# A hybrid encoder block: PSUM tiles of the w_o products, the rounding of the first key weights, and the place of the parameter transposes

## The chip, the cores and the metric

The kernel runs on one core of one Trainium2 chip. The metric is the device time of one execution in microseconds, lower is better. A core has TensorE (PE, matmuls; PEld is its loading of the stationary operand), VectorE (DVE), ScalarE (ACT), GpSimd (POOL) and SyncE (SP, which issues most of the DMAs). The engines run side by side, each works through its own queue in order, and they wait for each other on semaphores. TensorE accumulates in PSUM, in eight banks of 128 x 512 fp32.

## What is computed

One encoder block on x of 512 tokens by 1024 channels, all in fp32. Cut to what matters here:

```python
h = rmsnorm(x, norm1_w)
proj = h @ w_in              # pooling | q | k | v | z | beta, decay (the gate columns) | merge gates
...                          # pooling branch and gated delta rule over 8 heads, both directions
merged = sigmoid(g_pool) * y_pool + sigmoid(g_dn) * y_dn
x = x + merged @ w_o
h2 = rmsnorm(x, norm2_w)
u = dwconv_centered(h2 @ ffn_up, ffn_conv_w, ffn_conv_b)
gate, val = split(u)
return rmsnorm(x + (silu(gate) * val) @ ffn_down, final_norm_w)
```

## The kernel before

**Matmuls in three parts.** Every fp32 operand of the large products is split into a rounded high part (fp32r) and the rest, a low part. `mm3` (L388 to L391) issues three matmuls for each k-step of 128 rows: high x high (L389), and the two mixed ones (L390, L391). Weights come by DMA into a raw tile; in `weights` (L399 to L422) ScalarE rounds it (L411, one copy of 128 x 1024) and GpSimd subtracts, in two halves of 128 x 512 (L415).

**The order.** No engine's order is written out by hand. The kernel declares tasks (A for ScalarE, V for VectorE, G for GpSimd, M for TensorE, L for loads, Z for none), each with a cost, the names it reads and writes, and a key. A planner (L38) plays them through by costs and due keys and hands each engine its queue; after that the queues are fixed. Names such as `whi:k0#1` are parts of a buffer. Buffers of one tag form a ring: `pp` and `ds` have three PSUM banks each, `oo` is one tile of two banks (`banks2`, L307). Waits between engines are derived afterwards from the tiles that the instructions touch: instructions of different engines on one PSUM tile are kept in the order of the program.

**The head.** The first norm goes over four tiles of 128 tokens (`norm_transpose`, L526): ScalarE squares and sums a tile of x (L534), takes the root (L537), VectorE takes the reciprocal (L539) and scales it in two halves (L545), TensorE transposes each half into a `ds` bank (L556, four transposes), ScalarE rounds it into h_hi (L560), and VectorE subtracts into h_lo (L564), which frees the bank. The gate columns (L466, L467, L469) and the first two key heads (ps_k) are computed in two halves of 256 tokens, so that they can start on the first two tiles. Between these stand `par_turn` (L512), which transposes four blocks of small parameters (convolution weights, scales) into a `ds` bank, and `par_keep` (L517), by which ScalarE keeps them (cw, fw, small).

**The w_o stage.** merged @ w_o is computed by seven products of half size in place of eight (products 1, 2, 6, 5, 3, 7, 4 in this order). A product has 256 tokens, in two halves j of 128, and 512 rows (four k-steps) of 512 columns: 2 x 4 x 3 matmuls. Each half is accumulated in one PSUM bank and then added by VectorE to one or two quarters of x (`wplus`, L1776). Products 1 and 6 are also kept by ScalarE as wu (`wkeep`, L1783), product 1's for adding it into product 6 (`wmore`, L1788), product 6's for sums that GpSimd makes. The left operands are splits of merged (ms, L1566, L1570, L1657, L1661), the right ones splits of sums of w_o's quarters (L1617, L1630, L1633). Between product 4's k-steps stand the transposes of the second norm (pt_b, L1743), whose tiles come by L1727, L1729, L1730, L1733 and L1737. Behind it comes the FFN (ps_up).

The banks of the seven products, before, by `wname` and `wmm` (L1755 to L1766): products 1, 6, 3 and 4 share one tile wo of the ring `oo`, made once, with half j in its bank j; the halves of 2, 5 and 7 are tiles of the ring `pp`.

Of the kernel before, what the change touches and what calls it, by code (L numbers as in the profile page):

```python
# [205 lines left out]
def ca(n):  # L206
    return 0.22 + n * 0.00082
# [6 lines left out]
def cp(n):  # L214
    return 0.17 + n * 0.0023
# [12 lines left out]
def hybrid_block(  # L228
# [23 lines left out]
    pe, act, dve, pool, sp = nc.tensor, nc.scalar, nc.vector, nc.gpsimd, nc.sync  # L252
# [16 lines left out]
    def with_table(tab, fn):  # L269
        def run():  # L270
            if table["now"] != tab:
                table["now"] = tab
                if TABLES[tab]:
                    act.preload_act_table_set(TABLES[tab])
            fn()

        return run

    def A(cost, fn, r=(), w=(), key=0.0, tab=None):
        add("act", cost, with_table(tab, fn) if tab else fn, r, w, key, tab)  # L280
# [4 lines left out]
    def G(cost, fn, r=(), w=(), key=0.0, after=()):  # L285
        add("pool", cost, fn, r, w, key, after=after)

    def M(cost, fn, r=(), w=(), key=0.0, n=6):
        add("pe", cost, fn, r, w, key, n=n)

    def L(kb, fn, r=(), w=(), key=0.0, after=(), land=Planner.LAND, issue=Planner.ISSUE, eng="sp"):
        add(eng, issue, fn, r, w, key, kb=kb, after=after, land=land)
# [6 lines left out]
    FEED, EVICT, CHAIN = -3e6, -2e6, -1e6  # L299

    def f32(ap):
        return ap.bitcast(F32)

    def bank(tag, name):
        return psum.tile([P, 512], F32, tag=tag, bufs=RINGS[tag], name=name)

    def banks2(name, shape=(P, 2, 512)):  # L307
        return psum.tile(list(shape), F32, tag="oo", bufs=RINGS["oo"], name=name)
# [79 lines left out]
    def mm3(ps, ahi, alo, bhi, blo, first, last):  # L388
        pe.matmul(ps, ahi, bhi, start=first, stop=False)  # L389
        pe.matmul(ps, ahi, blo, start=False, stop=False)  # L390
        pe.matmul(ps, alo, bhi, start=False, stop=last)  # L391
# [3 lines left out]
    def next_unit():  # L395
        unit["n"] += 1
        return unit["n"] * 100.0

    def weights(src, kt, n, name, u, feed=None, more=0.0):  # L399
        feed = FEED + u if feed is None else feed  # L400

        b = {}

        def load():
            b["raw"] = wpool.tile([P, kt, n], F32, tag="wraw", bufs=RINGS["raw"], name=f"wr_{name}")
            sp.dma_start(b["raw"], src)

        def hi():
            b["hi"] = wpool.tile([P, kt, n], F32R, tag="whi", bufs=RINGS["whi"], name=f"wh_{name}")
            b["lo"] = wpool.tile([P, kt, n], F32R, tag="wlo", bufs=RINGS["wlo"], name=f"wl_{name}")  # L410
            act.copy(b["hi"], b["raw"])  # L411

        def lo(i):
            sl = slice(i * kt // 2, (i + 1) * kt // 2)
            pool.tensor_tensor(out=b["lo"][:, sl], in0=b["raw"][:, sl], in1=f32(b["hi"][:, sl]), op=ALU.subtract)  # L415

        whi, wlo = f"whi:{name}", f"wlo:{name}"
        L(kt * n * P * 4 / 1024, load, w=[f"raw:{name}"], key=feed)
        A(ca(kt * n), hi, r=[f"raw:{name}"], w=[whi, f"{wlo}#0"], key=feed)
        for i in range(2):  # L420
            G(cp(kt * n / 2) + more, lambda i=i: lo(i), r=[f"raw:{name}", whi], w=[f"{wlo}#{i}"], key=feed)
        return b, whi, wlo  # L422

    def job(src, kt, xs, xr, name, halves=False, pair=False, feed=None, more=0.0, at=None, turn=0):


        n = src.shape[1]
        u = next_unit()
        src = src.rearrange("(k p) c -> p k c", p=P)
        box = {}  # L430
        if pair:
            def load():
                box["raw"] = wpool.tile([P, kt, n], F32, tag="wraw", bufs=RINGS["raw"], name=f"wr_{name}")
                sp.dma_start(box["raw"], src)

            def split():
                w = box["hi"] = wpool.tile([P, kt, 2 * n], F32R, tag="whi", bufs=RINGS["whi"], name=f"wp_{name}")
                act.copy(w[:, :, 0:n], box["raw"])

            def split2():  # L440
                w = box["hi"]
                pool.tensor_tensor(out=w[:, :, n:], in0=box["raw"], in1=f32(w[:, :, 0:n]), op=ALU.subtract)

            whi = f"whi:{name}"
            wlo = whi
            L(128, load, w=[f"raw:{name}"], key=FEED + u)
            A(ca(kt * n), split, r=[f"raw:{name}"], w=[whi], key=FEED + u)
            G(cp(kt * n), split2, r=[f"raw:{name}"], w=[whi], key=FEED + u)
        else:
            if at:  # L450
                wk, wn = at(src, name, feed)
            else:
                wb, whi, wlo = weights(src, kt, n, name, u, feed, more)
                wk = lambda k: (wb["hi"][:, k, :], wb["lo"][:, k, :])
                wn = lambda k: [whi, f"{wlo}#{0 if k < kt // 2 else 1}"]
        pp = f"pp:{name}"

        def mmk(k, a, b):
            if "ps" not in box:
                box["ps"] = bank("pp", f"ps_{name}")  # L460
            xhi, xlo = xs(k)
            if pair:
                w = box["hi"]
                both = (box["ps"][: 2 * n, a:b], w[:, k, :], xhi[:, a:b])
                if k < kt - 1:
                    pe.matmul(*both, start=(k == 0), stop=False)  # L466
                pe.matmul(box["ps"][:n, a:b], w[:, k, 0:n], xlo[:, a:b], start=False, stop=False)  # L467
                if k == kt - 1:
                    pe.matmul(*both, start=False, stop=True)  # L469
                return  # L470
            mm3(box["ps"][:n, a:b], *wk(k), xhi[:, a:b], xlo[:, a:b], k == 0, k == kt - 1)

        spans = [(0, S)] if not halves else [(0, S // 2), (S // 2, S)]
        for i, (a, b) in enumerate(spans):
            for k in range(kt):
                M((MM3 if not pair else 0.46) / len(spans), lambda k=k, a=a, b=b: mmk(k, a, b),
                  r=([whi] if pair else wn(k)) + xr(k, a, b), w=[pp], key=u + (50 + turn) * i + k, n=4 if pair else 6)
        return box, pp, u
# [5 lines left out]
    par = {}  # L484
# [12 lines left out]
    def par_load(i):  # L497
        if "r" not in par:
            par["r"] = [pools["st"].tile([n, P], F32, name=f"par{i}") for i, n in enumerate((120, 88, 88, 5))]
        r = par["r"]  # L500
        (
            lambda: sp.dma_start(r[0], qkv_conv_w[0].rearrange("k (c p) -> (k c) p", p=P)),
            lambda: sp.dma_start(r[1], ffn_conv_w[0, 0:2].rearrange("k (c p) -> (k c) p", p=P)),
            lambda: sp.dma_start(r[2][0:44, :], ffn_conv_w[0, 2].rearrange("(c p) -> c p", p=P)),
            lambda: sp.dma_start(r[2][44:88, :], ffn_conv_b[0].rearrange("(c p) -> c p", p=P)),
            lambda: sp.dma_start(r[3][0:4, :], pool_scale[0].rearrange("(c p) -> c p", p=P)),
            lambda: sp.dma_start(r[3][4:5, :], dn_norm_w),
            lambda: sp.dma_start(ea, a_log[0].partition_broadcast(P)),
            lambda: sp.dma_start(dtb, dt_bias[0].partition_broadcast(P)),
        )[i]()  # L510
# [943 lines left out]
        )  # L1454
    for i in range(8):
        L(32, lambda i=i: par_load(i), w=[f"par#{i}"], key=FEED + 310 + i)
    M(0.6, par_turn, r=[f"par#{i}" for i in range(6)], w=["ds:par"], key=CHAIN, n=8)
    A(0.35, lambda: par_keep(0), r=["ds:par"], w=["cw"], key=CHAIN)
    A(0.6, lambda: par_keep(1), r=["ds:par"], w=["small"], key=CHAIN + 900)
    G(1.5, make_edges, w=["edges"], key=5000)  # L1460
# [51 lines left out]
    for c2 in range(KD // 2):  # L1512
# [9 lines left out]
      w=["wr"], after=["h"])  # L1522
# [63 lines left out]
    for t in range(NT):  # L1586
        L(512, lambda t=t: sp.dma_start(x2[t], xt[t * P : (t + 1) * P, :]), r=["pool:xp"], w=[f"xr{t}#0", f"xr{t}#1"],
          key=unit["n"] * 100, after=[f"pp:do{1 + t}"])
    L(512, lambda: sp.dma_start(pools["n2b"], norm2_w[0].partition_broadcast(P)), r=["pool:xp"], w=["n2b"],
      key=unit["n"] * 100, after=["pp:do5"])  # L1590
# [16 lines left out]
    for i, (kk, n) in enumerate(((0, 0), (0, 1), (2, 1), (1, 0), (1, 1), (3, 1), (2, 0), (3, 0))):  # L1607
        L(512, lambda n=n, kk=kk: wo_load(n, kk), r=["wr"], w=[f"wr{n}{2 * kk}", f"wr{n}{2 * kk + 1}"],
          key=WORK + u_w0, after=[f"pp:{pace[i]}"])
# [143 lines left out]
    wacc = {}  # L1753

    def wname(p, j):  # L1755
        return f"oo:wo#{j}" if p in (1, 6, 3, 4) else f"pp:wo{p}{j}"

    def wmm(p, k, j):
        name = wname(p, j)
        if p == 1 and "oo" not in wacc:  # L1760
            wacc["oo"] = banks2("wo")
        if name[0] == "p" and k == 0:
            wacc[name] = bank("pp", f"ps_wo{p}{j}")
        wacc[p, j] = wacc["oo"][:, j, :] if name[0] == "o" else wacc[name]
        a, ts_ = wsets[p], slice(j * P, (j + 1) * P)
        mm3(wacc[p, j], a[:, k, 0, ts_], a[:, k, 1, ts_], *wslot[p, k], k == 0, k == QK - 1)  # L1766

# [171 lines left out]
    for c in range(NF):  # L1939
        b = {}  # L1940
        for j in range(2):
            box, pp, u = first_jobs.get((c, j)) or up_job(c, j)
# [16 lines left out]
        else:  # L1959
            i = c - HK  # L1960
# [255 lines left out]
```

## Time and profile before

| | |
|---|---|
| median of 3 runs | 878.43 us (878.30 to 879.63) |
| the profiled execution's own time | 877.32 us |
| its span on the core | 875.5 us |
| TensorE busy | 863.7 us, 99% |
| VectorE, ScalarE, GpSimd busy | 592.0, 476.1, 530.1 us |
| granted TensorE clock, mean | 0.996 |
| moved by DMA | 138.09 MB, 158 GB/s |

The page shows one execution, by engine and by line of the kernel (L411 is line 411). In a row of the timeline stand the start and the duration in us, the engine, line and operation, the tiles as out<-in, shapes, and in brackets the idle time of the engine before it with what ended it. A row of the waits reads: who waited, for whom, us in total, times, longest. TensorE's matmuls overlap, so that 0.39 us is how long one is under way, and the distance between starts is what one costs.

### The profile page before, as it was taken

What the parts mean: (1) busy time and instruction counts of PE and PEld (TensorE: products, weight loads), DVE (VectorE), ACT (ScalarE), POOL (GpSimd) and SP (SyncE); (2) the same over time, 40 slices, a digit from 0 to 9 for tenths busy, and PEclk for the clock granted to TensorE, in tenths of its full rate; (3) what the DMA queues carried; (4) which work ended last, traced back from release to release, by engine and by line L of the source; (5) the groups of instructions that cost most, each with busy time, mean ns of one, the idle gap of its engine ahead of it and who ended that gap; (6) DMA issues with size and microseconds to landing.
All of it is one profiled execution on the core that took longest, in us unless ns stands there. A gap on an engine that the chain in (4) does not pass through costs nothing.

```text
span 875.5 us, 13895 instructions
## 1 busy us (share of the span) xinstructions
PE 863.7 (99%) x5051; PEld 730.5 (83%) x5051; DVE 592.0 (68%) x1040; ACT 476.1 (54%) x806; POOL 530.1 (61%) x459
## 2 busy tenths in 40 slices
PE   8999999999999999999999999999999999999997
PEld 7888888888888887889888789888888888888886
DVE  5756597367568897555676894656654555569996
ACT  6688544336858544345866664444443333455664
POOL 3445554324546654244597993778777887567663
PEclk9999999999999999999999999999999999999998
DMA  7365447304245463224898004666667666365553
GB/s 210 97 196 145 122 122 165 111 26 133 73 120 153 130 149 89 67 73 140 297 316 281 1 25 127 226 199 205 207 218 236 207 199 208 133 216 182 182 175 148
DMA packets 165512, 138.09 MB, mean 158 GB/s; under 512 B 23662, under 2 KB 133051, under 8 KB 165444
## 3 DMA queue, kind: packets, MB, share of 16 engines
q1 hardware_dynamic: 160706, 135.62, 50.5%
q10 hardware_dynamic: 4738, 1.58, 0.8%
q8 instruction: 40, 0.66, 0.3%
q14 instruction: 28, 0.23, 0.1%
HBM read 113.03 MB, written 24.15 MB: 157 GB/s over the span
## 4 chain that ended last, share of the span: by engine, by line
PE 97%; DVE 2%; ACT 0%; issue 0%; DVEq 0%
PE ps_up L389 9%; PE ps_up L391 9%; PE ps_up L390 9%; PE dn L391 4%; PE dn L389 4%; PE dn L390 4%; PE ps_k L389 2%; PE ps_gd L389 2%; PE ps_k L391 2%; PE ps_k L390 2%; PE pw L1167 2%; PE ps_q L391 2%; PE ps_q L389 2%; PE ps_v L390 2%; PE ps_gd L391 2%; PE ps_z L391 2%
## 5 line engine op out<-in xcount | busy, mean ns | idle before, releaser
L415 POOL TENSOR_TENSOR wl_up<-wr_up,wh_up 128x512 fp32r<-128x512 f32 x86 | 112.0, 1323 | 53.2 <-ACT wh_up L411 53.2
L389 PE MATMUL ps_up<-h_hi,wh_up 128*128 128x512 f32 (+1 forms) x360 | 136.8, 380 | 0.0
L390 PE MATMUL ps_up<-h_lo,wh_up 128*128 128x512 f32 (+1 forms) x360 | 136.6, 380 | 0.0
L391 PE MATMUL ps_up<-h_hi,wl_up 128*128 128x512 f32 (+1 forms) x360 | 136.6, 380 | 0.0
L1930 DVE SCALAR_TENSOR_TENSOR c<-ps_up,fw,c 128x511 f32<-128x511 f32 x88 | 66.0, 750 | 99.7 <-ACT c L1924 98.0
L2118 POOL TENSOR_TENSOR w_dn<-wr_dn,w_dn 128x512 fp32r<-128x512 f32 x44 | 65.8, 1509 | 28.8 <-ACT w_dn L2115 27.4
L391 PEld LDWEIGHTS ps_up<-h_hi,wl_up 128*128 128x128 f32 x360 | 67.7, 188 | 12.9
L390 PEld LDWEIGHTS ps_up<-h_lo,wh_up 128*128 128x128 f32 x360 | 67.7, 188 | 12.8
L389 PEld LDWEIGHTS ps_up<-h_hi,wh_up 128*128 128x128 f32 x360 | 67.7, 188 | 12.7
L411 ACT CAST wh_up<-wr_up 128x1024 fp32r<-128x1024 f32 x43 | 45.2, 1052 | 59.0 <-PE ps_up L390 23.4
L1915 POOL TENSOR_TENSOR tp<-tp 128x512 f32<-128x512 f32 x44 | 61.7, 1401 | 11.8 <-DMA tp<-in_ffn_down_dram 7.6
L2115 ACT CAST w_dn<-wr_dn 128x512 fp32r<-128x512 f32 x69 | 42.4, 621 | 29.5 <-PE dn L391 20.5
L390 PE MATMUL dn<-w_dn,as 128*128 128x512 f32 x141 | 54.2, 385 | 0.0
L389 PE MATMUL dn<-w_dn,as 128*128 128x512 f32 x141 | 54.2, 384 | 0.0
L391 PE MATMUL dn<-w_dn,as 128*128 128x512 f32 x141 | 54.2, 384 | 0.0
L1884 DVE TENSOR_TENSOR as<-a,as 128x512 fp32r<-128x512 f32 (+1 forms) x41 | 40.6, 1015 | 0.1
L1880 ACT CAST as<-a 128x512 fp32r<-128x512 f32 (+1 forms) x41 | 21.5, 534 | 33.4 <-DVE a L1950 29.8
L415 POOL TENSOR_TENSOR wl_k<-wr_k,wh_k 128x512 fp32r<-128x512 f32 x16 | 20.2, 1287 | 30.3 <-ACT wh_k L411 30.3
L1924 ACT ACTIVATE c<-ps_up,fw 128x512 f32<-128x512 f32 x44 | 33.9, 770 | 4.9 <-PE ps_up L391 4.9
L415 POOL TENSOR_TENSOR wl_v<-wr_v,wh_v 128x512 fp32r<-128x512 f32 x16 | 21.3, 1352 | 22.7 <-ACT wh_v L411 22.7
L415 POOL TENSOR_TENSOR wl_gp<-wr_gp,wh_gp 128x512 fp32r<-128x512 f32 x16 | 21.9, 1390 | 20.8 <-ACT wh_gp L411 20.8
L1952 ACT ACTIVATE c<-c 128x512 f32<-128x512 f32 x22 | 13.9, 632 | 33.0 <-DVE c L1930 33.0
(406 smaller groups left out, 2536.2 us busy)
## 6 DMA issues: line engine op xcount, KB each, us to landing
wr_up<-in_ffn_up_dram SPq DMA_DIRECT2D x44, 512.0 KB, 3.9
tp<-in_ffn_down_dram SPq DMA_DIRECT2D x22, 512.0 KB, 5.2
t_scr<-tp SPq DMA_DIRECT2D x44, 256.0 KB, 2.8
wr_dn<-t_scr SPq DMA_DIRECT2D x20, 512.0 KB, 3.7
wr_dn<-in_ffn_down_dram SPq DMA_DIRECT2D x15, 512.0 KB, 3.6
x<-in_x_dram SPq DMA_DIRECT2D x8, 512.0 KB, 5.4
wr_k<-in_w_in_dram SPq DMA_DIRECT2D x8, 512.0 KB, 4.7
wr_z<-in_w_in_dram SPq DMA_DIRECT2D x8, 512.0 KB, 3.8
```

The costliest lines, as they stand in the source:

```text
L389: pe.matmul(ps, ahi, bhi, start=first, stop=False)
L390: pe.matmul(ps, ahi, blo, start=False, stop=False)
L391: pe.matmul(ps, alo, bhi, start=False, stop=last)
L411: act.copy(b["hi"], b["raw"])
L415: pool.tensor_tensor(out=b["lo"][:, sl], in0=b["raw"][:, sl], in1=f32(b["hi"][:, sl]), op=ALU.subtract)
L1880: act.copy(sets[p][:, i : i + n, 0, :], src())
L1884: dve.tensor_tensor(out=w[:, :, 1, :], in0=src(), in1=f32(w[:, :, 0, :]), op=ALU.subtract)
L1915: G(cp(512), lambda o=o, x=x, y=y: pool.tensor_tensor(out=w(*o), in0=w(*x), in1=w(*y), op=ALU.subtract), r=[n(*x), n(*y)], w=[n(*o)], key=u)
L1924: act.activation(b[j], box["ps"], AF.Identity, scale=fw[:, 1, ci : ci + 1], bias=fw[:, 3, ci : ci + 1])
L1930: dve.scalar_tensor_tensor(out=y[:, lo:hi], in0=box["ps"][:, lo + sh : hi + sh], scalar=fw[:, k, ci : ci + 1], in1=y[:, lo:hi], op0=ALU.mu ...
L2115: act.copy(b["w"][:, 0, :], raw["t"][:, j, :])
L2118: eng.tensor_tensor(out=b["w"][:, 1, :], in0=raw["t"][:, j, :], in1=f32(b["w"][:, 0, :]), op=ALU.subtract)
```

## The change

Three things are edited. (1) The first key head's weights (k0) are rounded by GpSimd and not by ScalarE, in two halves, each followed by its subtraction; matmuls of the first four k-steps need the first halves alone. (2) The parameter transposes must wait until the first half of the last tile of the first norm is rounded (`h#hi30`). (3) Each half of each of the seven products has a PSUM tile of its own: 2, 5, 7 in `pp` as before, the first halves of 3 and 4 in `oo`, all others in `ds`.

```diff
         def hi():
             b["hi"] = wpool.tile([P, kt, n], F32R, tag="whi", bufs=RINGS["whi"], name=f"wh_{name}")
             b["lo"] = wpool.tile([P, kt, n], F32R, tag="wlo", bufs=RINGS["wlo"], name=f"wl_{name}")
-            act.copy(b["hi"], b["raw"])
+            if not first:
+                act.copy(b["hi"], b["raw"])
+
+        def hi_part(i):
+            sl = slice(i * kt // 2, (i + 1) * kt // 2)
+            pool.tensor_copy(out=b["hi"][:, sl], in_=b["raw"][:, sl])
...
+        first = name == "k0"
...
-        A(ca(kt * n), hi, r=[f"raw:{name}"], w=[whi, f"{wlo}#0"], key=feed)
+        (Z if first else A)(*(() if first else (ca(kt * n),)), hi, r=[f"raw:{name}"], w=[whi, f"{wlo}#0"], key=feed)
         for i in range(2):
-            G(cp(kt * n / 2) + more, lambda i=i: lo(i), r=[f"raw:{name}", whi], w=[f"{wlo}#{i}"], key=feed)
+            if first:
+                G(cp(kt * n / 2), lambda i=i: hi_part(i), r=[f"raw:{name}"], w=[f"{whi}#{i}"], key=feed)
+            G(cp(kt * n / 2) + more, lambda i=i: lo(i), r=[f"raw:{name}", f"{whi}#{i}" if first else whi], w=[f"{wlo}#{i}"], key=feed)
...
-                wn = lambda k: [whi, f"{wlo}#{0 if k < kt // 2 else 1}"]
+                wn = lambda k: [f"{whi}#{0 if k < kt // 2 else 1}" if name == "k0" else whi, f"{wlo}#{0 if k < kt // 2 else 1}"]
...
-    M(0.6, par_turn, r=[f"par#{i}" for i in range(6)], w=["ds:par"], key=CHAIN, n=8)
+    M(0.6, par_turn, r=["h#hi30", *(f"par#{i}" for i in range(6))], w=["ds:par"], key=CHAIN, n=8)
...
     def wname(p, j):
-        return f"oo:wo#{j}" if p in (1, 6, 3, 4) else f"pp:wo{p}{j}"
+        return f"{'pp' if p in (2, 5, 7) else 'oo' if p in (3, 4) and not j else 'ds'}:wo{p}{j}"
 
     def wmm(p, k, j):
         name = wname(p, j)
-        if p == 1 and "oo" not in wacc:
-            wacc["oo"] = banks2("wo")
-        if name[0] == "p" and k == 0:
-            wacc[name] = bank("pp", f"ps_wo{p}{j}")
-        wacc[p, j] = wacc["oo"][:, j, :] if name[0] == "o" else wacc[name]
+        if k == 0:
+            wacc[p, j] = banks2(f"wo{p}")[:, 0, :] if name[0] == "o" else bank(name[:2], f"ps_wo{p}{j}")
```

Behind `weights` the lines of the changed kernel are numbered 8 higher, behind `wmm` 5 higher. The planner's order moves in the head alone. On ScalarE, in the first norm, before (wh_k is the rounded weight of k0, pt_a the transposes, xs and nst_a the scaled tile and its statistics):

```order
L438 CAST wp_gate<-wr_gate 128x8x32
L560 CAST h_hi<-pt_a_0_241 128x4x128
L411 CAST wh_k_258<-wr_k_201 128x1024
L560 CAST h_hi<-pt_a_1_251 128x4x128
L560 CAST h_hi<-pt_a_0_263 128x4x128
L560 CAST h_hi<-pt_a_1_271 128x4x128
L534 ACTIVATE xs_281,nst_a_282<-x_2_207 128x1024
```

and now, in the same place of ScalarE's queue:

```order
L446 CAST wp_gate<-wr_gate 128x8x32
L568 CAST h_hi<-pt_a_0_241 128x4x128
L568 CAST h_hi<-pt_a_1_251 128x4x128
L568 CAST h_hi<-pt_a_0_264 128x4x128
L542 ACTIVATE xs_278,nst_a_279<-x_2_207 128x1024
L568 CAST h_hi<-pt_a_1_272 128x4x128
L545 ACTIVATE nst_a_279<-nst_a_279,eps_t 128x1
```

The rounding of the weights is gone from it, and the square of tile 2 has moved ahead of the fourth rounding of h. On GpSimd, now, behind the gate's weights (wl_k is the low part):

```order
L450 TENSOR_TENSOR wp_gate<-wr_gate,wp_gate 128x8x32
L365 AFFINE_SELECT mask<-mask 128x128
L416 CAST wh_k_257<-wr_k_201 128x512
L420 TENSOR_TENSOR wl_k_258<-wr_k_201,wh_k_257 128x512
L416 CAST wh_k_257<-wr_k_201 128x512
L420 TENSOR_TENSOR wl_k_258<-wr_k_201,wh_k_257 128x512
L960 MEMSET ext_384 32x4x4x32
```

where before the two subtractions stood alone. TensorE's queue in the head is interleaved anew: ahead of tile 2's transposes it has now eight gate matmuls, three k-steps of the key and six gate matmuls, and the parameter transposes come behind the last transposes of the norm, before the key's last k-step of the first half.

In the w_o stage each engine's order is the same as before, with other tiles. TensorE from product 1's first half into its second, before, with the semaphores that a row waits for:

```order
L391 MATMUL wo<-ws_hi_4620,ms_4629 128x512
L389 MATMUL wo<-ws_hi_4581,ms_4629 128x512
L390 MATMUL wo<-ws_lo_4582,ms_4629 128x512
L391 MATMUL wo<-ws_hi_4581,ms_4629 128x512
L389 MATMUL wo<-ws_hi_4586,ms_4629 128x512 [waits Activation_49]
L390 MATMUL wo<-ws_lo_4587,ms_4629 128x512
```

and now:

```order
L391 MATMUL ps_wo_4942<-ws_hi_4621,ms_4630 128x512
L389 MATMUL ps_wo_4972<-ws_hi_4582,ms_4630 128x512
L390 MATMUL ps_wo_4972<-ws_lo_4583,ms_4630 128x512
L391 MATMUL ps_wo_4972<-ws_hi_4582,ms_4630 128x512
L389 MATMUL ps_wo_4972<-ws_hi_4587,ms_4630 128x512
L390 MATMUL ps_wo_4972<-ws_lo_4588,ms_4630 128x512
```

The second half has another tile than the first, and its second k-step waits for no other engine any more.

## The prediction

> **What bounds the kernel now.** I read the page first: TensorE is busy for 99% of the span, and the chain that ended last runs over it for 97%.
>
> ```profile
> span 875.5 us, 13895 instructions
> PE 863.7 (99%) x5051; PEld 730.5 (83%) x5051; DVE 592.0 (68%) x1040; ACT 476.1 (54%) x806; POOL 530.1 (61%) x459
> ...
> PE 97%; DVE 2%; ACT 0%; issue 0%; DVEq 0%
> ```
>
> The change takes away no matmul, so it can win only time in which TensorE stands still. The waits of TensorE list all of it:
>
> ```profile
> PE wo L389 <- ACT wu L1783: 2.1, 2, 1.4
> PE pt_warm L595 <- DVE ones L334: 1.1, 1, 1.1
> PE pt_a L556 <- DVE xs L545: 0.9, 1, 0.9
> PE l1a L999 <- DVE ext L966: 0.5, 1, 0.5
> PE ps_gate L467 <- DVE h_lo L564: 0.4, 1, 0.4
> PE ps_gate L466 <- ACT h_hi L560: 0.4, 1, 0.4
> ```
>
> That is 5.4 us. The first row is the w_o stage, and the last two are the first norm; the change touches these three. The second and third come before any changed instruction, the fourth lies in the triangular inverse. So the ceiling is about 3 us of 878, and the question is how much of it comes back as a wait for something else. TensorE's timeline (columns: start, duration) at the two w_o waits:
>
> ```profile
> 481.77 0.39 PE L390 MATMUL wo<-ws_lo,ms 128*128 128x512 f32 x1
> 482.00 0.39 PE L391 MATMUL wo<-ws_hi,ms 128*128 128x512 f32 x1
> 483.79 0.50 PE L389 MATMUL wo<-ws_hi,ms 128*128 128x512 f32 x1 [1.40 <-ACT wu L1783]
> 484.13 0.39 PE L390 MATMUL wo<-ws_lo,ms 128*128 128x512 f32 x1
> ...
> 502.37 0.40 PE L391 MATMUL ps_wo<-wq_kT,ms 128*128 128x512 f32 x1
> 503.51 0.50 PE L389 MATMUL wo<-ws_hi,ms 128*128 128x512 f32 x1 [0.74 <-ACT wu L1783]
> 503.84 0.40 PE L390 MATMUL wo<-ws_lo,ms 128*128 128x512 f32 x1
> ```
>
> Matmuls of 512 columns start every 0.23 us. The first wait costs 483.79 - 482.00 - 0.23 = 1.56 us, and the restart another 484.13 - 483.79 - 0.23 = 0.11. The second costs 503.51 - 502.37 - 0.23 = 0.91 and again about 0.10. Together **2.68 us**.
>
> **The w_o stage, what goes.** The matmul at 483.79 is the second k-step of product 1's second half. It writes bank 1 of the tile wo, but the copy that it waits for reads bank 0:
>
> ```profile
> 482.42 0.69 DVE L1776 TENSOR_TENSOR x<-wo,x 128x512 f32<-128x512 f32 x1
> 483.15 0.59 ACT L1783 COPY wu<-wo 128x512 f32<-128x512 f32 x1 [2.82 <-DVE x L1776]
> 484.79 0.62 ACT L1630 CAST ws_hi<-wr_lo 128x512 fp32r<-128x512 f32 x1 [0.54 <-PE wo L391]
> 485.32 0.37 ACT L1566 CAST ms<-ps_do 128x256 fp32r<-128x256 f32 x1
> 486.80 0.42 DVE L1570 TENSOR_TENSOR ms<-ps_do,ms 128x256 fp32r<-128x256 f32 x1
> ...
> 502.87 0.59 ACT L1783 COPY wu<-wo 128x512 f32<-128x512 f32 x1 [0.98 <-DVE x L1776]
> ```
>
> Both halves are one tile, so the order puts bank 1 behind it: 483.15 + 0.59 = 483.74, matmul at 483.79. The second wait is the same copy for product 6 (502.87 + 0.59 = 503.46, matmul at 503.51); product 3 writes into that tile next. With a tile for each half both are gone: product 3's first half takes the ring oo, whose last tile, of the delta rule, is long out of use, and the ds and pp rings come round to banks of two products earlier.
>
> **What is late next.** Product 2's fourth k-step needs the last d_o column's split, ACT L1566 and DVE L1570, which ends at 487.22. TensorE now gets there at 486.3 (its high part) and 486.8 (the low part), 1.67 earlier. ACT L1566 stood behind the cast at 484.79, which itself waited 0.54 us for the delayed matmuls; without that it ends at about 485.1 and the chain behind it moves up by 0.6, to 486.6. That is in time by 0.2 us.
>
> Further on the transposes of the second norm, put between product 4's k-steps, are next. Their chain runs over VectorE:
>
> ```profile
> 497.20 0.70 DVE L1788 TENSOR_TENSOR wo<-wo,wu 128x512 f32<-128x512 f32 x1 [1.00 <-PE wo L391]
> 509.28 0.69 DVE L1776 TENSOR_TENSOR x<-wo,x 128x512 f32<-128x512 f32 x1 [0.55 <-PE wo L391]
> 514.10 0.95 DVE L1733 SCALAR_TENSOR_TENSOR sq<-x,nst,n2b 128x512 f32<-128x512 f32 x1
> 515.21 0.49 PE L1743 MATMUL pt_b<-ident,sq 128*128 128x128 f32 x3
> ...
> 497.00:503.00 6.00, 5.76 (x25) 4.32 (x23) 5.74 (x7) 3.24 (x8) 5.64 (x5) 1.00 0.00 0
> 503.00:509.30 6.30, 5.79 (x25) 4.80 (x26) 5.75 (x9) 4.30 (x8) 6.30 (x5) 1.00 0.00 0
> 509.30:515.00 5.70, 5.70 (x27) 4.69 (x25) 5.59 (x7) 4.37 (x9) 5.70 (x5) 1.00 0.00 0
> ```
>
> (Windows: length, then busy time and count of PE, PEld, DVE, ACT, POOL.) The scaled row is ready at 515.05 and TensorE takes it at 515.21: 0.16 us of slack, on an engine that is busy for 17.1 of these 18.0 us. TensorE will ask 2.68 us earlier. VectorE wins the 1.00 us at 497.20 (the sum of product 6's first half waited there for its second half, by the shared tile) and the 0.55 at 509.28 (product 3, the same). It also starts its splits for product 5 earlier: their buffer is free when product 2's matmuls end, 1.67 us sooner, of which ScalarE's queue and the subtractions ahead (moved up 0.6) let through about 1.2. That makes 2.7 to 2.8, just what TensorE gains. As such a sum is no better than some tenths, I let 0.2 us come back. The w_o stage gives **2.5 us**; bounds 1.5 (only the two idle stretches are won) and 2.7.
>
> GpSimd is full as well in these windows. But the waits of TensorE hold no row on GpSimd, and its queue moves up too, with ScalarE's casts that it splits; I put nothing on it.
>
> **The head.** ScalarE's rounding of the first key weights, which stood between the tiles of the first norm, goes to GpSimd:
>
> ```profile
> 9.69 1.05 ACT L411 CAST wh_k<-wr_k 128x1024 fp32r<-128x1024 f32 x1
> 10.64 1.56 ACT L560 CAST h_hi<-pt_a 128x512 fp32r<-128x512 f32 x3
> 12.07 1.09 ACT L534 ACTIVATE xs<-x 128x1024 f32<-128x1024 f32 x1
> ...
> 8.08 3.39 PE L556 MATMUL pt_a<-ident,xs 128*128 128x128 f32 x16 [0.93 <-DVE xs L545]
> 12.60 0.30 PE L467 MATMUL ps_gate<-h_lo,wp_gate 128*32 128x256 f32 x1 [0.44 <-DVE h_lo L564]
> ...
> 13.81 1.41 DVE L545 SCALAR_TENSOR_TENSOR xs<-x,nst_a,n1b 128x512 f32<-128x512 f32 x2
> 16.65 1.28 DVE L564 TENSOR_TENSOR h_lo<-pt_a,h_hi 128x512 fp32r<-128x512 f32 x2
> ...
> 8.63 0.30 POOL L365 TENSOR_SCALAR_AFFINE_SELECT mask<-mask 128x128 f32<-128x128 f32 x1
> 10.82 2.52 POOL L415 TENSOR_TENSOR wl_k<-wr_k,wh_k 128x512 fp32r<-128x512 f32 x2 [1.89 <-ACT wh_k L411]
> ```
>
> The 1.05 us are not all won, since the transposes (0.21 us each) end the second group at 10.0 and the third at 10.9. The third h_hi then ends at 11.5 instead of 11.7, its h_lo at 12.2, and the first gate matmul that needs both starts at 12.28 instead of 12.60: 0.32 won. But the square of tile 2 (1.09 and the reading of its sum) now stands ahead of the fourth h_hi. That ends at 13.2 instead of 12.2, VectorE's fourth h_lo at 13.95, and the scaling of tile 2, which began at 13.81, begins at 14.2: 0.4 later. TensorE comes for it at 14.9 (8 gate matmuls, 9 of the key, 6 of the gate from 12.28 on, at 0.12, half of a 512-column one), and waits 0.1 us. The fourth pair of transposes needs a ds buffer that tile 2's first h_lo frees: 17.8 instead of 17.3, with TensorE there at 17.6, 0.2 us more. By the same count the last gate matmul ends 0.1 us later than before. The parameter transposes cost TensorE the same at their new place; it did not wait for their loads at the old one, and the first reader of cw comes only when the whole first key head is accumulated. The head gives **-0.1 us**; from +0.35 (no new wait) to -0.5 (each wait twice as long).
>
> GpSimd's rounding of 128x512 is in no row. From below it is bounded by the 0.52 us in which GpSimd only writes as much per partition, from above by its subtraction, 2.52 / 2 = 1.26 us, which reads two operands and rounds too; I take 1.2, as rounding is the part that they share. The weights have landed at 9.69 at the latest, GpSimd is free at 8.93, so that the four parts end at 10.9, 12.2, 13.4 and 14.7 at the latest. TensorE wants the first pair at 13.1 and 13.4, the second at 17.0. It costs nothing up to 2.3 us for one rounding.
>
> ```profile
> 18.75 0.52 POOL L952 MEMSET ext<- 32x512 f32 x1 [5.40 <-ACT h_hi L560]
> ```
>
> [...]
>
> **Sum.** 2.5 - 0.1 = 2.4 us. The profiled execution's own time of 877.32 us would be 874.9; the median of the runs shown, 878.43, lies 1.1 above that execution, and becomes **876.0**. A measurement of this kernel can tell 0.2%, 1.76 us, from no change.
>
> **Rivals.**
> *VectorE becomes the bound at the second norm.* If it wins only the 1.00 and 0.55 us of idle, TensorE waits 2.68 - 1.55 - 0.16 = 1.0 us at the first transposes of product 4, and the change is worth 1.6: 876.8, no change by the bound. For it speaks how full both engines are, and that VectorE's splits vary with what GpSimd does:
>
> ```profile
> L1661 DVE TENSOR_TENSOR ms<-m,ms x8: 685/1638/1780, 487.3 to 511.6; 128x512 fp32r<-128x512 f32 x8
> ```
>
> 685 ns when alone, 1.64 to 1.78 us beside GpSimd; if one or two of the early, short ones fall beside GpSimd, the chain loses 1 us. [...]
> *The head wins its 0.35 and no new wait comes*: 2.68 + 0.35 = 3.0, 875.4.
> *Nothing comes of it*: the halves still wait for each other, 878.4. The order shows no such wait left.
> *Slower: GpSimd's rounding is slow code.* From 2.3 us on TensorE waits for it. At 5 us the first low part comes at 9.0 + 5 + 1.3 = 15.3 instead of 13.3, the last at 21.6 against 17.0 + 2.0: 4.6 us lost, 2.2 slower in all, 880.6. Every GpSimd row that rounds speaks against it.
>
> **Chances.** Forecast 0.54, VectorE 0.25, head 0.10, nothing 0.05, slow rounding 0.06. Of the forecast 0.02 lies short of 1.76. Faster 0.62, within 0.2% 0.32, slower 0.06. The range begins at 875.2, the head's case less the 0.2 by which runs differ at the lower end, and reaches 877.9, the VectorE case with the head's -0.5 and half of the runs' spread of 1.3; left out are the last two.
>
> **What would show it.** Right: no wait of TensorE on a copy of wu in the w_o stage; product 2 starting 1.67 us closer to product 1 and product 4 2.7 us; the first gate pair at 12.3 and GpSimd's roundings near 1.2 us. Wrong: a wait at pt_b for VectorE over 0.5 us, at ps_do's split in product 2, for whi on GpSimd in the head, or a first gate half that ends over 0.5 us later.

## The result, and the profile after

The changed kernel ran in 876.45 us (median of 8 runs, 875.13 to 879.20), the one before beside it in 879.44 (8 runs, 878.30 to 881.84): ratio 0.9966, 95% interval 0.9950 to 0.9981. It is faster, by 3.0 us in this comparison and by 2.0 in the two later ones (0.9974 and 0.9975). The profiled execution took 876.64 us, with a span of 874.8. Its page, then the waits of TensorE:

```profile
span 874.8 us, 13894 instructions
PE 865.2 (99%) x5051; PEld 731.2 (84%) x5051; DVE 596.7 (68%) x1040; ACT 475.3 (54%) x805; POOL 531.1 (61%) x461
```

```profile
PE pt_warm L603 <- DVE ones L334: 1.1, 1, 1.1
PE pt_a L564 <- POOL wp_gate L450: 0.9, 1, 0.9
PE pkq L1098 <- ACT qT L794: 0.5, 1, 0.5
PE l1a L1007 <- DVE ext L974: 0.5, 1, 0.5
```

The row on wu is gone, and so are the two of the first norm. New is pkq, the first key-query product at 294 us, which no edit touches. TensorE's timeline at the two places where it stood before:

```profile
483.36 0.39 PE L391 MATMUL ps_wo<-ws_hi,ms 128*128 128x512 f32 x1
483.59 0.39 PE L389 MATMUL ps_wo<-ws_hi,ms 128*128 128x512 f32 x1
483.82 0.39 PE L390 MATMUL ps_wo<-ws_lo,ms 128*128 128x512 f32 x1
...
502.05 0.39 PE L391 MATMUL ps_wo<-wq_kT,ms 128*128 128x512 f32 x1
502.28 0.39 PE L389 MATMUL wo<-ws_hi,ms 128*128 128x512 f32 x1
502.51 0.40 PE L390 MATMUL wo<-ws_lo,ms 128*128 128x512 f32 x1
```

All starts are 0.23 us apart. Put beside the same matmuls of before (482.00, 483.79, 484.13 and 502.37, 503.51, 503.84 in the prediction's rows), they start 1.36 later, 0.20 earlier, 0.31 earlier, and then 0.32, 1.23 and 1.33 earlier. So 1.67 and 1.01 us are won, 2.68 together, as worked out. But TensorE comes 1.36 us late to this stage, and the whole span is only 0.7 shorter. Two questions follow: what made it late (the change, or the run), and what of the 2.7 us is kept.

For that I matched TensorE's instructions of each profile with those of before and took the difference of the starts at five places. Counted from the last matmul ahead of the first wait (before at 482.00), in us, negative is won:

| kernel of the profile | behind wait 1 | behind wait 2 | behind tile 1's transposes and product 4 (520) | behind the up product's first low weights (535) |
|---|---|---|---|---|
| changed, three profiles | -1.69, -1.69, -1.69 | -2.70, -2.69, -2.72 | -2.39, -2.37, -2.39 | -2.06, -2.04, -2.06 |
| w_o tiles alone, two profiles | -1.69, -1.69 | -2.72, -2.71 | -2.38, -2.41 | -2.06, -2.06 |
| changed, eight roundings | -1.69 | -2.69 | -2.36 | -2.05 |
| product 1 alone | -1.69 | -1.44 | -1.42 | -1.42 |
| next late moved | -1.69 | -2.71 | -2.59 | -2.24 |
| one addition less | -1.69 | -2.72 | -2.59 | -2.59 |
| before again | -0.01 | 0.00 | 0.01 | 0.01 |

Within the stage the trace repeats to 0.03 us, while whole runs of one kernel spread over 4 us. The stage is worth **2.06 us**, and 0.64 of the 2.70 come back in two halves of 0.32.

### The profile page after: what moved, and what is told of

Same layout as the page of the kernel before. It is cut to its first block, busy times and chain, and to the rows that moved or that the text cites. A ratio compares the mean times of both kernels' runs of the same rounds, so it can differ in the third digit from the quotient of the medians.

```text
span 874.8 us, 13894 instructions
## 1 busy us (share of the span) xinstructions
PE 865.2 (99%) x5051; PEld 731.2 (84%) x5051; DVE 596.7 (68%) x1040; ACT 475.3 (54%) x805; POOL 531.1 (61%) x461
## 4 chain that ended last, share of the span: by engine, by line
PE 60%; POOL 3%; DVE 2%; issue 1%; ACT 1%; DVEq 0%; POOLq 0%
PE ps_up L391 9%; PE ps_up L389 9%; PE ps_up L390 9%; PE dn L391 4%; PE dn L389 4%; PE dn L390 4%; PE ps_do L389 2%; PE ps_do L390 2%; PE ps_do L391 2%; PE ps_gp L389 1%; PE ps_gp L391 1%; PE ps_gp L390 1%; PE ps_p L389 1%; PE ps_po L391 1%; PE ps_po L389 1%; PE ps_po L390 1%
```

## The experiments

Theory A: the gain is the two w_o waits, with little given back. B: half or more comes from the head. C: VectorE becomes the bound at the second norm. D, formed on the way: a full queue, GpSimd's above all, gives a part of every gain back.

**1. The w_o tiles alone.** The diff's third edit on the kernel before.

```diff
-        return f"oo:wo#{j}" if p in (1, 6, 3, 4) else f"pp:wo{p}{j}"
+        return f"{'pp' if p in (2, 5, 7) else 'oo' if p in (3, 4) and not j else 'ds'}:wo{p}{j}"
...
```

> The kernel before with the PSUM tiles of the w_o products alone; every engine's order is that of before. Theory A (the gain is the two waits of TensorE on the copies wu, and little comes back): no TensorE wait on wu; product 4 starts 2.5 to 2.7 us closer to product 1 than the 35.7 us of before, up to 0.5 us comes back behind it; time 0.24% to 0.30% under before (ratio 0.9970 to 0.9976). Theory B (half or more of the measured 0.34% is the head's): the w_o tiles alone give 0.15% or less. Theory C (VectorE becomes the bound at the second norm): a TensorE wait of 0.7 us or more at pt_b or just behind, gain 0.2% or less.

Measured: median 878.26, ratio 0.9989 [0.9978, 1.0000], short of theory A's 0.9970 to 0.9976. The profile shows the stage's 2.06 us, the runs about 1.1. Its TensorE reaches 482 us 3.59 us later than in the first profile of before, so the runs, not the stage, had to be looked at (experiments 5 and 9).

**2. The head alone.** The first two edits, and the banks as before; against the changed kernel:

```diff
-        return f"{'pp' if p in (2, 5, 7) else 'oo' if p in (3, 4) and not j else 'ds'}:wo{p}{j}"
+        return f"oo:wo#{j}" if p in (1, 6, 3, 4) else f"pp:wo{p}{j}"
...
```

> The kernel before with GpSimd's rounding of the first key weights and the later parameter transposes, the w_o tiles as before. Theory A: about nothing, ratio 0.9990 to 1.0010; from the first transpose of the norm to the 30th us TensorE is within 0.4 us of before; the w_o waits of 1.56 and 0.91 us stand as before. Theory B: 0.15% to 0.2% faster, with the gate's matmuls and all behind them 1 us or more earlier, counted from the norm's first transpose.

Measured: 878.90, ratio 0.9996 [0.9986, 1.0006]; not to be told from no change. The waits on wu are those of before (2.2 us in two).

**3. The rounding eight times over.**

```diff
-            pool.tensor_copy(out=b["hi"][:, sl], in_=b["raw"][:, sl])
+            for _ in range(8):
+                pool.tensor_copy(out=b["hi"][:, sl], in_=b["raw"][:, sl])
```

> The changed kernel with each of GpSimd's two roundings of the first key weights done eight times over (same values). One takes 0.61 us in the profile after, so that a half costs 4.9 us in place of 0.6. By the count in the prediction (free up to 2.3 us for a half; at 5 us 2.0 us lost ahead of the first low part and 2.6 ahead of the second) the kernel is 4 to 5 us slower than the changed one, about 0.5%, and TensorE's waits show whi or wl of the key on GpSimd for as much. If the key's first matmuls are not what the head hangs on, it costs under 1 us.

Measured: 882.46, ratio 1.0027 [1.0017, 1.0038], 5.1 us above the changed kernel of the same chip (877.35). GpSimd's timeline and two of TensorE's waits:

```profile
8.84 5.38 POOL L417 CAST wh_k<-wr_k 128x512 fp32r<-128x512 f32 x8
14.30 1.27 POOL L421 TENSOR_TENSOR wl_k<-wr_k,wh_k 128x512 fp32r<-128x512 f32 x1
```

```profile
PE ps_k L391 <- POOL wl_k L421: 1.7, 2, 0.9
PE ps_k L389 <- POOL wh_k L417: 0.5, 1, 0.5
```

Eight roundings take 5.38 us, and TensorE leaves the head 4.75 us later than in the changed kernel's first profile (5.09 against 0.34 behind before, at 280 us; the clock of the two heads differs: this one has a second stretch at half clock, 0.50, from 15.7 to 19.1 us). The slower rival priced one rounding of 5 us at 4.6 lost. Its arithmetic holds to some tenths; only its condition doesn't, since one rounding is short:

```profile
9.00 0.61 POOL L416 CAST wh_k<-wr_k 128x512 fp32r<-128x512 f32 x1
9.70 1.28 POOL L420 TENSOR_TENSOR wl_k<-wr_k,wh_k 128x512 fp32r<-128x512 f32 x1
```

(The changed kernel.)

**4. The changed kernel again,** without an edit.

> The changed kernel unchanged, on the same chip as the others. Its first profile shows a TensorE wait of 0.7 us at pkq near 294 us, behind a round trip of rw through DRAM, and a slower clock in the warming-up matmuls, which the profile before does not have. If both are chance from run to run, this profile lacks one or both, its span comes below 874.3 us and the ratio is 0.9955 to 0.9975; if the change causes them they are here again, at the same places with the same size within 0.2 us.

Measured: 877.35, ratio 0.9974 [0.9964, 0.9984]. The stage is the same to 0.02 us, but this profiled execution took 879.09 us, 2.5 more than the first of the same kernel; 2.1 of that it has at 280 us. Its first transposes start at 10.82 us, where those of the first profile start at 8.88.

**5. Before again,** unchanged.

> The kernel before once more, unchanged, for a second profile of it. In every profile taken since, TensorE waits 0.04 to 1.0 us at the first key-query product at about 294 us (pkq, for ScalarE's qT), which the first profile of before does not show. Theory A (the gain is that of the two w_o waits; this wait and the place of the half-clock stretch in the head vary from run to run whatever the kernel): this profile shows the pkq wait too, or a half-clock stretch elsewhere in the first 20 us, with an own time 0 to 3 us above the first profile's 877.3; the two waits on wu are again 1.56 and 0.91 us, to within 0.1; the median lies within 0.5 us of the 879.4 of the other runs of before. Rival B (the changed head brings the pkq wait): no wait at pkq here.

Measured: 879.84, ratio 0.9999 [0.9991, 1.0008]; the profiled execution took 881.34 us, and its waits have this row:

```profile
PE pkq L1090 <- ACT qT L786: 0.8, 1, 0.8
```

This run's rival (the changed head brings the pkq wait) falls: the wait at 294 us is there without the change. All thirteen profiles taken after the first one of before have 0.3 to 1.6 us of delay at this place; the first has none. And it leaves the head 2.35 us later. Of the 1.36 us by which the changed kernel came late to the w_o stage it has 0.34 at 280 us, 0.76 at this place and 0.27 between there and the stage. The last two are of the run: experiments 6 and 9, whose heads are that of before, have both as well. The 0.34 lie in the head, which is taken up below. The profile on which the prediction rests was of a lucky execution: 877.32 us, where the fastest of 116 runs of before took 877.47 and their median is 879.50.

**6. Product 1 alone** in tiles of its own; 6, 3 and 4 share one as before.

```diff
-        return f"oo:wo#{j}" if p in (1, 6, 3, 4) else f"pp:wo{p}{j}"
+        return f"ds:wo1{j}" if p == 1 else f"oo:wo#{j}" if p in (6, 3, 4) else f"pp:wo{p}{j}"
...
```

> The kernel before, with only product 1's two halves in tiles of their own; products 6, 3 and 4 share the tile wo as before. Theory A: the first wait on wu (1.67 us with its restart) goes, the second stays at 0.9 to 1.0, and nothing comes back, since GpSimd's last low weights had 1.6 us to spare before TensorE in the profile of before; the last w_o matmul is 1.6 to 1.7 us closer to the first than before; ratio 0.998 to 0.9985. Theory D (a queue that is full, GpSimd or VectorE, gives back part of every gain from the first us on): under 1.2 us, and a new wait of TensorE between product 1 and the up product.

Measured: 877.69, ratio 0.9985 [0.9974, 0.9995]. The first wait goes, 1.69; the second grows:

```profile
PE wo L389 <- ACT wu L1783: 1.0, 1, 1.0
```

It idled 0.74 before. TensorE is 1.69 early ahead of this wait and 1.44 behind it: 0.25 us come back there, and nothing after it. Neither A nor D forecast this: not all is kept, and no new wait took the rest, but the old one that was left.

**7. What is late next, moved.** Product 4's second half goes to `pp`, and GpSimd takes the first half of the up product's second low weights ahead of the square of tile 3, the second half behind it.

```diff
-            G(cp(kt * n / 2) + more, lambda i=i: lo(i), r=[f"raw:{name}", f"{whi}#{i}" if first else whi], w=[f"{wlo}#{i}"], key=feed)
+            G(cp(kt * n / 2) + more, lambda i=i: lo(i), r=[f"raw:{name}", f"{whi}#{i}" if first else whi], w=[f"{wlo}#{i}"], key=feed + (0.7 * i if name == "up0_1" else 0))
...
-        G(cp(512), weigh, r=[f"xr{t}#{hf}", "n2b"], w=[sqn(t, 0)], key=u)
+        G(cp(512), weigh, r=[f"xr{t}#{hf}", "n2b"], w=[sqn(t, 0)], key=WORK + u_wo[4] + 51.5 if t == 3 else u)
...
-        return f"{'pp' if p in (2, 5, 7) else 'oo' if p in (3, 4) and not j else 'ds'}:wo{p}{j}"
+        return f"{'pp' if p in (2, 5, 7) or (p, j) == (4, 1) else 'oo' if p in (3, 4) and not j else 'ds'}:wo{p}{j}"
```

> The changed kernel with the two waits that its own profile shows behind the w_o products taken away: product 4's second half goes to the pp ring instead of the ds ring (whose buffer VectorE frees late, 0.17 us lost), and GpSimd takes the first half of the up product's second low weights ahead of the square of tile 3 instead of behind it (0.35 us lost at 523.8 to 524.2). Theory A with these two as the whole give-back: from the second k-step of product 1's second half to the up product TensorE is 0.3 to 0.5 us closer than in the changed kernel, 2.3 to 2.6 closer than in the one before; in time 0.0 to 0.6 us under the changed kernel, not to be told from it, ratio to before 0.9965 to 0.9975. Rival (the full queue only hands the wait on): the two waits go and one on the second half of the same low weights, or at the transposes of tile 3, of 0.3 us or more takes their place.

The two waits that it is aimed at, in the changed kernel's list of all engines between 515 and 526 us (the weight loads, PEld, carry them):

```profile
PEld ps_up L391 <- POOL wl_up L420: 0.3, 1, 0.3
PEld ps_wo L389 <- DVE h_lo L1758: 0.2, 1, 0.2
```

and in this kernel's between 515 and 535:

```profile
PEld ps_up L391 <- POOL wl_up L420: 0.3, 1, 0.3
PEld pt_b L1751 <- DVE sq L1741: 0.2, 1, 0.2
```

Measured: 876.45, ratio 0.9966 [0.9954, 0.9978]; by the profile 0.18 better than the changed kernel (2.24 against 2.06), less than the 0.3 to 0.5 expected, and far too little for the runs to show. The `ds` bank's 0.19 us are won. The wait for GpSimd is not: it went from the first half of these weights to the second. The rival was right for that half. Reordering this queue, which has no idle time there, only chose who waits.

**8. The rounding alone,** the first edit without the others.

```diff
-            act.copy(b["hi"], b["raw"])
+            if not first:
+                act.copy(b["hi"], b["raw"])
...
+            if first:
+                G(cp(kt * n / 2), lambda i=i: hi_part(i), r=[f"raw:{name}"], w=[f"{whi}#{i}"], key=feed)
...
```

> The kernel before with only the rounding of the first key weights moved to GpSimd; the parameters stay ahead of the last transposes, the w_o tiles are as before. If the head's 0.3 to 0.5 us comes from ScalarE's relief (theory B's part), the first gate matmul and all behind it start 0.3 to 0.6 us earlier, against the start of the first transposes, than in before, and the median is 0.3 to 0.8 us under before's (ratio 0.9990 to 0.9997). If it comes from the parameter transposes, this kernel is at before's time within 0.2 us (ratio 0.9998 to 1.0002), which an interval of 0.001 can't tell from the first; the profile has to.

**9. The w_o tiles alone, again,** the kernel of experiment 1.

> The kernel of the first experiment once more (the w_o halves in tiles of their own, the head as before), since its median of 878.26 shows 1.1 us of the 2.0 that its profile shows. Theory A (the 2.0 are real, runs of one kernel differ by up to 4 us through the head's clock): the profile again loses two waits of 1.63 and 0.93 and takes back 0.2 at product 4's second half and 0.35 at the up product, 2.0 net, nothing more lost behind 531 us; median 877.0 to 878.0, and the mean of all 22 runs 1.4 to 2.0 under before's. Rival: something behind 531 us takes a part back in runs that were not profiled: median again 878.2 or more.

**10. The parameters alone,** the second edit without the others.

```diff
-    M(0.6, par_turn, r=[f"par#{i}" for i in range(6)], w=["ds:par"], key=CHAIN, n=8)
+    M(0.6, par_turn, r=["h#hi30", *(f"par#{i}" for i in range(6))], w=["ds:par"], key=CHAIN, n=8)
```

> The kernel before with only the parameter transposes put behind the first norm's last split. The prediction gave the move nothing. Against a profile of before with the same clock the key product behind the head starts within 0.1 us of it; ratio 0.9995 to 1.0005. Rival (the transposes stood in the way of the fourth tile's): 0.2 to 0.4 us earlier, ratio 0.9993 to 0.9998; the profile has to tell the two.

Measured: 8 at 879.09, ratio 0.9994 [0.9984, 1.0003]; 9 at 877.54, 0.9977 [0.9967, 0.9987]; 10 at 879.28, 0.9998 [0.9988, 1.0007]. In 9 nothing is lost behind 535 us (-2.06 at 535, -2.05 at 863), so that the small gain of experiment 1 can be put down to scatter; the mean of its 23 runs is 877.93 against 879.54 for the 116 of before, 1.61 less (standard errors 0.23 and 0.09); the profile's 2.06 is within two of these. For 10 the profile decides: its half-clock stretch lies within 0.1 us of that of before, and TensorE leaves the head 0.06 earlier. The transposes cost nothing at either place.

For 8 there is a like match with experiment 6, whose head is that of before. In both the granted clock (the third number from the end) is halved from 9.9 to 13.3 us. Experiment 6, then 8:

```profile
10.00:13.00 3.00, 2.92 (x13) 2.02 (x11) 2.91 (x5) 2.43 (x4) 1.52 (x2) 0.50 1.02 271
13.00:16.00 3.00, 2.72 (x20) 1.99 (x18) 1.83 (x5) 2.93 (x6) 1.00 (x1) 0.94 0.34 78
```

```profile
10.00:13.00 3.00, 2.92 (x13) 2.02 (x11) 2.97 (x5) 2.20 (x4) 2.57 (x3) 0.50 1.01 278
13.00:16.00 3.00, 3.00 (x25) 2.74 (x25) 2.13 (x5) 2.48 (x7) 0.00 (x0) 0.94 0.23 44
```

From 10 to 13 both do the same 13 matmuls; from 13 to 16 the second does 25 and the first 20. ScalarE's, VectorE's and TensorE's rows of experiment 6:

```profile
10.35 1.05 ACT L411 CAST wh_k<-wr_k 128x1024 fp32r<-128x1024 f32 x1
13.04 0.59 ACT L560 CAST h_hi<-pt_a 128x512 fp32r<-128x512 f32 x1 [0.61 <-PE pt_a L556]
13.52 1.07 ACT L534 ACTIVATE xs<-x 128x1024 f32<-128x1024 f32 x1
...
15.23 1.41 DVE L545 SCALAR_TENSOR_TENSOR xs<-x,nst_a,n1b 128x512 f32<-128x512 f32 x2
...
16.12 0.63 PE L556 MATMUL pt_a<-ident,xs 128*128 128x128 f32 x4 [0.35 <-ACT xs L534]
```

and of experiment 8:

```profile
12.32 1.06 ACT L542 ACTIVATE xs<-x 128x1024 f32<-128x1024 f32 x1
13.38 0.58 ACT L568 CAST h_hi<-pt_a 128x512 fp32r<-128x512 f32 x1
...
14.78 1.40 DVE L553 SCALAR_TENSOR_TENSOR xs<-x,nst_a,n1b 128x512 f32<-128x512 f32 x2
...
15.86 0.60 PE L564 MATMUL pt_a<-ident,xs 128*128 128x128 f32 x4
```

With the transposes slow, at a granted clock of 0.50, the fourth rounding of h can't start before 13.04, and in the old queue the square of tile 2 stands behind it, until 13.52. The new queue has the square ahead: 1.20 us earlier, tile 2 scaled 0.45 earlier, its transposes 0.26, and TensorE doesn't wait there. At 280 us the first is 1.35 behind the profile of before, the second 0.55: **0.80 us** for the rounding, under this clock.

**11. One addition less** on GpSimd, with product 4's second half in `pp`. Left out is the sum of product 6's kept copy (not product 5's part) into the first half of tile 2, so that the output isn't the block's.

```diff
-        return f"{'pp' if p in (2, 5, 7) else 'oo' if p in (3, 4) and not j else 'ds'}:wo{p}{j}"
+        return f"{'pp' if p in (2, 5, 7) or (p, j) == (4, 1) else 'oo' if p in (3, 4) and not j else 'ds'}:wo{p}{j}"
...
-            e.tensor_tensor(out=dst, in0=src(), in1=dst, op=ALU.add)
+            (eng is G and n == j == 0) or e.tensor_tensor(out=dst, in0=src(), in1=dst, op=ALU.add)
```

> The changed kernel with product 4's second half in the pp ring, and with one 1.3 us addition of GpSimd left out ahead of the up product's low weights (product 5's part in tile 2, so that x2 lacks it there). If GpSimd's full queue is what gives time back (theory D at this one place), no wait on wl_up is left: from the first wait on wu to the up product TensorE gains all of 2.6 to 2.7 us against before, 0.3 to 0.4 more than with the queue's order changed, and 0.6 to 0.7 more than in the changed kernel. If VectorE or the ds bank gives it back, 0.2 us or more is still lost between 517 and 531 us.

Measured: 876.38, ratio 0.9967 [0.9954, 0.9980]. With 1.3 us less in GpSimd's queue the wait on wl_up is gone and nothing comes in its place: 2.59 kept at 520 and still 2.59 at 535. GpSimd's share of what comes back is thereby shown; the 0.13 left at tile 1's transposes are VectorE's.

**12. The changed kernel, a third time,** without an edit.

> The changed kernel a third time, beside the two parts. Theory A with the head's 0.3 to 0.9 us (where the half-clock stretch lies over the norm's transposes): median 876.4 to 877.4, ratio 0.9966 to 0.9978, and the mean over all its runs 2.3 to 2.9 us under before's, the sum of the two parts' means to within 0.6. If the parts interact, the sum of the parts misses it by more.

Measured: 877.09, ratio 0.9975 [0.9964, 0.9987]. Over its 30 runs the changed kernel's mean is 877.15 (standard error 0.21), 2.39 under before. The parts give 1.61 and, for the head (its 11 runs: 878.90), 0.64: 2.25. They add up. Against the w_o tiles alone the changed kernel is 0.78 faster, with a standard error of 0.31: the head's worth in time, known to a few tenths at best (the means differ by 0.99 on the chip of experiments 1 and 4, by 0.25 on that of 9 and 12). Theory B's half or more is not borne out; it is about a third.

## Why the prediction came out right, and where its steps failed

The sum, 2.4 us, is what the runs show (2.39, standard error 0.23), but that it fits so well is luck: its two terms were each off and made up for each other. The stage gave 2.06 by the trace in place of 2.5, the head 0.3 to 0.8 in place of -0.1.

**The two waits**: 1.67 and 1.01 as worked out, in every profile with the edit. The two products start closer as said. Product 2's fourth k-step came in time: the 1.69 stand unchanged from 484 to 502 us.

**VectorE at the second norm**: right in kind, a little short in size. I let 0.2 come back; it is 0.32, 0.13 at tile 1's transposes and 0.19 at the bank of product 4's second half, which h_lo frees late. At the first tile, where I looked for it, there is none. The rival's 1.0 us did not come, nor theory C's 0.7.

**"GpSimd ... I put nothing on it"** is a step that failed. 0.32 us. The reason I gave, that its queue moves up with ScalarE's casts, holds for a part only. Before, then after, GpSimd at the last idle time that both have, at the two that only before has behind it, and at the low weights, and TensorE at the first matmul on these:

```profile
488.89 3.19 POOL L1633 TENSOR_TENSOR ws_lo<-wr_lo,ws_hi 128x512 fp32r<-128x512 f32 x2 [1.50 <-PE ps_wo L391]
501.31 2.58 POOL L1718 TENSOR_TENSOR sq<-x,n2b 128x512 f32<-128x512 f32 x2 [0.36 <-ACT sq L1715]
518.23 1.29 POOL L1718 TENSOR_TENSOR sq<-x,n2b 128x512 f32<-128x512 f32 x1 [0.33 <-ACT sq L1715]
521.98 2.57 POOL L415 TENSOR_TENSOR wl_up<-wr_up,wh_up 128x512 fp32r<-128x512 f32 x2
...
524.95 0.28 PE L391 MATMUL ps_up<-h_hi,wl_up 128*128 128x256 f32 x1
```

```profile
489.60 1.50 POOL L1641 TENSOR_TENSOR ws_lo<-wr_lo,ws_hi 128x512 fp32r<-128x512 f32 x1 [0.81 <-ACT ws_hi L1638]
522.77 2.57 POOL L420 TENSOR_TENSOR wl_up<-wr_up,wh_up 128x512 fp32r<-128x512 f32 x2
...
523.80 0.28 PE L390 MATMUL ps_up<-h_lo,wh_up 128*128 128x256 f32 x1
524.15 0.39 PE L391 MATMUL ps_up<-h_hi,wl_up 128*128 128x256 f32 x1
```

Against the stage's start, which lies 1.37 later, the idle time that both have ends 0.66 earlier and the weights come 0.58 earlier, while TensorE comes 2.39 earlier. The two later idle times, 0.69 us together, are gone as well, but nothing is left of them: the same 22 instructions take 33.17 us (489.60 to 522.77) in place of 32.40 (488.89 to 521.98 less 0.69), 0.77 more. All but one take about 1.3 or about 1.75 us each, and 12 take the longer time in place of 10; why, no run here settles. So the full queue moved up by 0.66 + 0.69 - 0.77 = 0.58. The first half of the weights, ready at about 521.98 + 1.28 = 523.26, had 1.7 us to spare before. Without a wait TensorE would now be there at 524.95 + 1.37 - 2.39 = 523.93, the weights at 522.77 + 1.28 = 524.05; it goes on at 524.15, with a first matmul of 0.39 us where the others take 0.28. That the waits of TensorE held no row on GpSimd said only that there was some slack, not how much. The rows for the count were in the trace.

**The head, -0.1**, is the other. By the runs it is worth 0.6 to 0.8, with standard errors of 0.3; by the profiles 0.3 to 0.8, as the clock falls. Two things failed. The first is to have taken one execution's clock as given. Granted clock (third number from the end) from 7 to 13 us, before:

```profile
7.00:10.00 3.00, 2.07 (x10) 1.95 (x10) 2.77 (x5) 1.63 (x6) 0.98 (x2) 0.58 1.09 372
10.00:13.00 3.00, 2.17 (x14) 1.47 (x13) 2.45 (x5) 3.00 (x5) 2.18 (x2) 0.85 1.03 275
```

In the profile of before the half-clock stretch of 3.4 us is over at 10.9, when the third group of transposes ends, and the old queue suffers little. In most others it lies later. By where it starts (summed from the granted clock in half-microsecond windows) and TensorE's delay at 280 us against the profile of before; in brackets the same counted from the first transposes, which start at 8.08 there and at 8.03 to 10.82 in the others:

| head | start of the stretch: delay, us |
|---|---|
| of before | 7.5: 0; 8.2: 0.39 (0.05); 9.9: 1.35 (0.23); 10.2 and 10.3, to 17.0 and 17.1: 2.35 and 2.39 (1.10 and 1.08) |
| parameters alone | 7.4: -0.06 (-0.01) |
| rounding alone | 9.9: 0.55 (-0.57) |
| changed | 9.2: 0.34 (-0.46); 9.5 and 9.6: 0.46 and 0.48 (-0.48 both); none on record: 2.44, 2.45, 2.46 (-0.30, -0.29, -0.28) |

Behind the first transposes a late stretch costs the old head up to 1.1 us; the new one, which met none later than 9.9, loses nothing. How often each place comes up is not settled.

The second is the price itself, which was wrong under the old clock too. The three changed heads with no stretch on record meet the transposes at the same pace as the profile of before, 16 in 3.44 us against 3.39. Experiment 4:

```profile
10.82 3.44 PE L564 MATMUL pt_a<-ident,xs 128*128 128x128 f32 x16 [0.93 <-POOL wl_k L420]
14.14 1.06 ACT L542 ACTIVATE xs<-x 128x1024 f32<-128x1024 f32 x1
15.02 0.30 PE L475 MATMUL ps_gate<-h_lo,wp_gate 128*32 128x256 f32 x1 [0.33 <-DVE h_lo L572]
16.60 1.41 DVE L553 SCALAR_TENSOR_TENSOR xs<-x,nst_a,n1b 128x512 f32<-128x512 f32 x2
17.64 0.60 PE L564 MATMUL pt_a<-ident,xs 128*128 128x128 f32 x4
```

Less the 2.74 us by which the first transposes come later, the first gate pair starts at 12.28, as forecast, and TensorE comes to tile 2's transposes at 14.90, as counted. But the square of tile 2 starts at 11.40 (12.07 before), and the scaling of tile 2 at 13.86: 0.05 later than before, not 0.4. Neither of the two waits, 0.1 and 0.2 us, is there. So this head wins 0.28 to 0.30 us, close to the 0.35 that the prediction gave for the head without a new wait; the step that failed is the 0.4 for the square's new place and the waits put on it. One sign that was named for a miss did come, a first gate half that ends over 0.5 us later: its last matmul starts at 18.20 - 2.74 = 15.46 against 14.26. That is the new order alone, with nine key matmuls and tile 2's first transposes ahead of it, and delays nothing.

**GpSimd's rounding** took 0.61 us, not 1.2; it was free up to 2.3, so that nothing hung on it. **The parameters** cost nothing, as put. **The median** of 876.0 went by 878.43 for before; 879.50 over 116 runs less the same 2.4 would have been 877.1, where the 30 runs have 876.96.

## What to carry to other kernels

When a wait is taken from the bounding engine, count for each producer behind it how far that producer's own queue moves up: one that is full until the place moves up by the idle time it had and no more, less what its instructions grow by, and takes back whatever exceeds its slack (here GpSimd, 0.58 us for TensorE's 2.39, of which 0.32 came back). A wait that only a shared tile makes is cheap to split, but the gain is the idle time minus what is late next (here 2.70 less 0.64 us). And where an execution has a clock stretch that falls elsewhere each time (here its start lay between 7.4 and 10.3 us), take the stage's distances from the trace, the worth from many runs, and compare two heads from their first common instruction under a like clock.

## What the runs showed of the hardware

**The clock at the start.** How fast TensorE works in the first 10 us differs from run to run, and some of that isn't in the granted clock. The 22 warm-up matmuls and the 4 behind them, in the profile of before and in the second of the changed kernel (experiment 4); the clock reads 1.00 over all of these rows in both:

```profile
1.12 4.12 PE L595 MATMUL pt_warm<-ones 128*128 128x128 f32 x22 [1.12 <-DVE ones L334]
5.17 1.98 PE L586 MATMUL n1b<-n1row,ones 1*128 1x512 f32 x4
```

```profile
1.12 5.06 PE L603 MATMUL pt_warm<-ones 128*128 128x128 f32 x22 [1.12 <-DVE ones L334]
6.11 3.78 PE L594 MATMUL n1b<-n1row,ones 1*128 1x512 f32 x4
```

The last four take 3.78 us in place of 1.98, about half the rate: they end 6.11 + 3.78 - 5.17 - 1.98 = 2.74 us later, and as late come the first transposes. With the stretch's place this makes up to 2.5 us of delay at 280 us in these profiles; whole runs of one kernel spread over 4 us, and the wait at pkq, with its 0.3 to 1.6 us of delay, has a part in that too. The stretch, with a granted clock of 0.50, lasts 3.4 us in before (7.5 to 10.9), after (9.2 to 12.6) and experiment 6 (9.9 to 13.3). In experiments 1 and 5 it lasts twice as long, 6.8 us (10.3 to 17.1 and 10.2 to 17.0). Why the granted clock falls from 1.00 to 0.50 for this time, no run here shows.

**GpSimd's rounding,** with one input, of 128 x 512 took 0.61 us in the changed kernel, where its subtraction with two takes 1.28 in the head, 2.1 times as long (up to 1.76 in the w_o stage); VectorE's subtraction for h_lo, of the same size, takes 0.68.
